# Gate stage of a two-layer encoder: its set-up and first two slices written inside the down projection's last group, and the gate product's first and last slices written in pairs

## The chip, the cores and the metric

The kernel runs on one core of one Trainium2 chip. The metric is the device time of a whole execution in microseconds (us), as the median of several runs.

## The reference

Two layers of an encoder block act on x, 1024 tokens of width 1024. Cut to what the kernel's stages need:

```
h = rmsnorm(x, g_pre_mix)
proj = h @ w_in                        # split in q, k, v, u, ... parts
y = concat(diff_attention(...), spatial_gating(b_u, b_v, ..., w_spatial, ...),
           window_gqa(...)) @ w_out
x = x + rmsnorm(y, g_post_mix)
gate, up = split(rmsnorm(x, g_pre_ffn) @ w_ffn_in)
f = (silu(gate) * up) @ w_ffn_out      # the down projection, 2816 -> 1024
x = x + rmsnorm(f, g_post_ffn)
e = p @ w_ple_up                       # p: 1024 x 256
g = sigmoid(rmsnorm(x, g_ple_gate) @ w_ple_gate)      # the gate product
x = x + rmsnorm(e * g, g_ple_post)
```

The gate stage is all that stands from the norm of f to the last line. It is run once in each layer.

## The kernel before

**Numbers.** Everything is float32. A product is made of three matmuls with the operands split into a high part (fp32r) and a low part (the rest): high x high, high x low, low x high. The two parts of an operand come from two instructions: ACT writes the high part (L209 for activations, L161 for weights, L819 for gate weights), VectorE subtracts it from the source and writes the low part (L210, L162, L820).

**Tiling.** The 1024 tokens are eight slices t of 128 rows. `T(t)` holds a slice in row form. `to_X` (L205) turns a slice into column form for use as a matmul's stationary operand: for each half of 512 columns it makes four transposes on TensorE into one bank of banks 4 to 7 (L202), then L209 and L210 read that bank. Which bank is taken is decided when the kernel is built: the one taken longest ago.

**The gate stage** (L807 to L884). Its set-up loads two gains, the column gain `gcol` and eight blocks of gate weights (L818), and converts them (L819, L820) into six tiles of pool W and two of pool F. For each slice the generator `ple` (L848) then has these steps:

- the norm of f (L850, with rows L194, L187, L189, L196), the load of the slice of x1 into `gv[:, 2]` (L852), the residual sum (L853), and the scaled copy `h1` (L855, L856);
- `to_X(h1)` (L858);
- the gate product `gmm(t)` (L864), its sigmoid on ACT (L866), the load of the slice of e into `gv[:, 3]` (L868), product (L869), norm, and the sum into `T(t)` (L871); then the store to x3 and, in layer 0, the norm for the next layer;
- in layer 0, `to_X(h2)` for the next layer's input (L880).

`gv[:, 2]` and `gv[:, 3]` are one buffer each: a slice's load waits until the slice before has been read. `gmm` is built by `rows_mm` (L223). When a slice is first asked for, it takes two banks of 0 to 3 and makes 48 matmuls of 128x512: for k from 0 to 7 six of them (L220), on two halves, with weight tile k.

**Around it.** Ahead stands the down projection: 11 groups c of two units, each over eight slices and two halves (L799), added by L805 into `T(t)`. Behind layer 0's gate stands the next layer's input product, called wb: the spatial weights are loaded into a buffer of the pool `raw` (L329) and turned by four transposes (L334). Eight blocks of w_in are loaded into `raw` (L173, three DMAs each) and converted into W (six) and F (two); `bmm` (L340) is the product by `rows_mm`. The projections (L238) come behind it.

**What sets the order.** The kernel isn't written in engine order. A scheduler simulates the program when it is built, hoists an instruction when its inputs and buffers are free, and fixes one order for each engine; the engines then run their rows strictly as they stand and wait on semaphores. The order in which the code is written is a priority, and it also decides the cycling of buffers and banks. Pools have a fixed number of buffers: W 6, F 2, raw 2, A 7, P 4, G 2.

Of the kernel before, what the change touches and what calls it, by code (L numbers as in the profile page):

```python
# [11 lines left out]
F32 = mybir.dt.float32  # L12
# [45 lines left out]
def encoder_kernel(  # L58
# [123 lines left out]
    def rows_unit(tag, w, k, eng=nc.vector, r=None, to=None):  # L182
        return unit(tag, lambda r: [(r, w[k * P : (k + 1) * P, :])], eng, r, to)
# [33 lines left out]
    def rows_step(ps, x, units, k, halves=(0, 1)):  # L217
        for a, b in ((0, 0), (0, 1), (1, 0)):
            for hf in halves:
                nc.tensor.matmul(ps[:, hf], x[a][:, k * P : (k + 1) * P], units[k][b][:, hf * 512 : (hf + 1) * 512],  # L220
                                 start=(k == 0 and a == 0 and b == 0), stop=(k == len(units) - 1 and a == 1))

    def rows_mm(units, x):  # L223
        done = {}

        def get(t):
            if t not in done:
                done[t] = pbank2()
                for k in range(len(units)):
                    rows_step(done[t], x(t), units, k)  # L230
            return done[t]

        return get
# [8 lines left out]
    def ple_prep(l, tags):  # L242
        pT = [pair("P") for _ in range(2)]
        for hf in range(2):
            pr = new(tags[hf], [P, 4, PLE])
            nc.sync.dma_start(pr, p[l, 0, hf * 512 : (hf + 1) * 512, :].rearrange("(t p) c -> p t c", p=P))
            for k in range(2):
                pp = pbank()
                for t in range(4):
                    nc.tensor.transpose(pp[:, t * P : (t + 1) * P], pr[:, t, k * P : (k + 1) * P], ident)  # L250
                hi = pT[k][0][:, hf * 512 : (hf + 1) * 512]
                nc.scalar.activation(hi, pp, AF.Copy)
                nc.vector.tensor_tensor(pT[k][1][:, hf * 512 : (hf + 1) * 512], pp, hi.bitcast(F32),
                                        op=ALU.subtract)
# [47 lines left out]
    for l in range(DEPTH):  # L302
# [34 lines left out]
        wb = wb if l == 0 else []  # L337
        while len(wb) < KT:
            wb.append(load_wb(l, len(wb)))
        bmm = rows_mm(wb, xt)  # L340
        V = region()

        def vt(t, c0, n):
# [438 lines left out]
                pass  # L782

        T = rows_regions()
        for c in range(ND // 2):
            if l > 0:
                if c == 1:
                    up = ple_prep(l, "GG")
                if 2 <= c < 2 + NT:
                    ple_up(l, c - 2, *up, "G")  # L790
            ds = (2 * c, 2 * c + 1)
            fs = [unit("FW"[c % 2], lambda r: [(r, f_d[l][d].rearrange("p a c -> p (a c)"))]) for d in ds]
            ws = [rows_unit("W", wfo, d) for d in ds]
            for t in range(NT):
                for hf in range(2):
                    po = pbank(range(8))
                    for i in range(2):
                        for a, b in ((0, 0), (0, 1), (1, 0)):
                            nc.tensor.matmul(po, fs[i][a][:, t * P : (t + 1) * P], ws[i][b][:, hf * 512 : (hf + 1) * 512],  # L799
                                             start=(i == 0 and a == 0 and b == 0), stop=(i == 1 and a == 1))  # L800
                    acc = T(t)[:, hf * 512 : (hf + 1) * 512]
                    if c == 0:
                        nc.scalar.activation(acc, po, AF.Copy)
                    else:
                        nc.vector.tensor_tensor(acc, po, acc, op=ALU.add)  # L805

        X, xt = x_regions()  # L807
        gv = region()
        gpo = gain("G", g_post_ffn, l)
        gcol = sb.tile([P, KT], F32, tag="gcol", name=nm("gcol"), bufs=1)  # L810
        nc.sync.dma_start(gcol, g_ple_gate[l].rearrange("(k p) -> p k", p=P))
        gpp = gain(None, g_ple_post, l, gv[:, 0])
        gnx = gain(None, g_pre_mix, l + 1, gv[:, 1]) if l + 1 < DEPTH else None
        wg = []
        for k in range(KT):

            r, w = new("raw", [P, 1024]), pair("W" if k < 6 else "F")
            nc.sync.dma_start(r, w_ple_gate[l, k * P : (k + 1) * P, :])  # L818
            nc.scalar.activation(w[0], r, AF.Copy, scale=gcol[:, k : k + 1])  # L819
            nc.vector.scalar_tensor_tensor(w[1], r, gcol[:, k : k + 1], w[0].bitcast(F32),  # L820
                                           op0=ALU.mult, op1=ALU.subtract)
            wg.append(w)
        gmm = rows_mm(wg, xt)

        def ple_tail(t):
            e, eg, y = gv[:, 1], new("G", [P, DM]), new("P", [P, DM])
            nc.sync.dma_start(e, e_d[l][t])
# [52 lines left out]
                to_X(h2, xt(t))  # L880
            yield

        for _ in skew(ple, NT, (2, 1, 0, -1)):
            pass  # L884


# [45 lines left out]
```

## Time and profile before

| | us |
|---|---|
| runs before, three: lowest, median, highest | 2720.49, 2721.49, 2722.28 |
| the profiled execution's own time | 2721.15 |
| its span on the profile's page | 2719.4 |
| gate product and wb product, TensorE busy in L220 with weights in W (1728 matmuls) | 419.5 |
| the same with weights in F (576 matmuls) | 148.1 |
| down projection, TensorE busy in L799 (both forms) | 263.7 and 220.0 |

The page describes one execution. It gives each engine's busy time, a chain of the work that ended last, and the costliest groups of instructions; further views show the rows of an engine in order of time, each with its start, its duration and, in brackets, the idle time ahead of it and what ended that, and the busy time of all engines in chosen windows. PE is TensorE, PEld its weight loads, DVE is VectorE, SP issues the DMAs. PEclk is the clock that TensorE was granted, 1.00 being full speed.

### The profile page before, as it was taken

To read this page: it belongs to the slowest core of one execution; us is meant where nothing else is said; L and a number is where in the kernel's file an instruction comes from. 1 tells how busy PE (TensorE), PEld (TensorE's weight loads), DVE (VectorE), ACT (ScalarE), POOL (GpSimd) and SP (SyncE) were. 2 spreads that over 40 slices of the span, in tenths; PEclk is the share of its full clock that TensorE was granted. 3 is DMA by queue.
4 is the path that set the end of the run, shared out by engine and by line. 5 is a ranking of instruction groups with operands and counts; after the bars stand their busy time and mean duration, and the time that the engine had idled before them with its cause. 6 is when DMAs were issued, how large, how long until landed. Compare 5 with 4: busy or idle time off the path is not lost.

```text
span 2719.4 us, 35553 instructions
## 1 busy us (share of the span) xinstructions
PE 2660.4 (98%) x13760; PEld 2140.7 (79%) x13760; DVE 1757.5 (65%) x2992; ACT 1143.2 (42%) x1911; POOL 319.3 (12%) x299
## 2 busy tenths in 40 slices
PE   8999999999999999999999999989999999999998
PEld 6887776778888888887878777668788888888877
DVE  5237698678666656767632677966866666466684
ACT  6126687543222223214521577854522222321253
POOL 1002335210000000001100223532000000000010
PEclk9999999999999999999999999999999999999999
DMA  6153402133232314334224323112323232332342
GB/s 238 28 155 92 110 2 71 71 95 94 85 93 71 93 69 150 99 101 136 93 82 116 94 71 93 30 57 86 101 93 93 70 93 74 132 125 104 132 131 78
DMA packets 193466, 258.38 MB, mean 95 GB/s; under 512 B 26513, under 2 KB 142737, under 8 KB 193297
## 3 DMA queue, kind: packets, MB, share of 16 engines
q1 hardware_dynamic: 193296, 256.11, 30.4%
q8 instruction: 108, 1.77, 0.3%
q14 instruction: 62, 0.50, 0.1%
HBM read 195.25 MB, written 60.82 MB: 94 GB/s over the span
## 4 chain that ended last, share of the span: by engine, by line
PE 91%; DVE 4%; ACT 2%; issue 1%; DMA 1%; POOL 1%; SPq 0%; DVEq 0%; POOLq 0%; ACTq 0%
PE banks L720 30%; PE banks L220 18%; PE banks L799 17%; PE banks L238 8%; PE banks L515 3%; PE banks L487 3%; PE banks L509 3%; PE banks L202 2%; PE banks L266 2%; PE banks L419 1%; PE banks L444 1%; PE banks L435 1%; PE banks L521 1%; DVE A L196 1%; DVE P L490 1%
## 5 line engine op out<-in xcount | busy, mean ns | idle before, releaser
L720 PE MATMUL banks<-A,W 128*128 128x512 f32 x3072 | 710.3, 391 | 7.4 <-ACT W L161 4.6
L720 PEld LDWEIGHTS banks<-A,W 128*128 128x128 f32 x3072 | 579.1, 189 | 131.4 <-ACT W L161 5.8
L220 PE MATMUL banks<-W,A 128*128 128x512 f32 x1728 | 419.5, 396 | 10.2 <-ACT A L209 6.0
L220 PEld LDWEIGHTS banks<-W,A 128*128 128x128 f32 x1728 | 324.3, 190 | 79.6 <-ACT A L209 7.3
L805 DVE TENSOR_TENSOR A<-banks,A 128x512 f32<-128x512 f32 x320 | 213.9, 687 | 109.6 <-PE banks L799 109.3
L799 PE MATMUL banks<-W,F 128*128 128x512 f32 x1152 | 263.7, 389 | 0.0
L799 PEld LDWEIGHTS banks<-W,F 128*128 128x128 f32 x1152 | 216.2, 188 | 44.9
L799 PE MATMUL banks<-W,W 128*128 128x512 f32 x960 | 220.0, 389 | 1.8 <-ACT W L161 1.8
L161 ACT ACTIVATE W<-G 128x1024 fp32r<-128x1024 f32 x88 | 92.5, 1060 | 296.7 <-PE banks L720 278.9
L189 POOL TENSOR_TENSOR stats<-stats,neghalf 128x1 f32<-128x1 f32 (+1 forms) x112 | 84.8, 759 | 1114.6 <-DVE stats L187 1113.8
L799 PEld LDWEIGHTS banks<-W,W 128*128 128x128 f32 x960 | 180.1, 188 | 39.4 <-ACT W L161 2.0
L161 ACT ACTIVATE W<-raw 128x1024 fp32r<-128x1024 f32 x92 | 96.6, 1060 | 208.6 <-PE banks L799 102.1
L238 PE MATMUL banks<-A,F 128*128 128x512 f32 x768 | 183.4, 393 | 0.0
L744 DVE TENSOR_TENSOR P<-banks,P 128x512 f32<-128x512 f32 x44 | 30.4, 691 | 219.8 <-PE banks L720 219.8
L238 PEld LDWEIGHTS banks<-A,F 128*128 128x128 f32 x768 | 142.3, 188 | 29.3 <-ACT G L428 0.3
L490 DVE CUSTOM_DVE_ANT_0 P<-banks,dist 128x1024 f32<-128x1024 f32 x116 | 139.8, 1219 | 32.5 <-PE banks L487 19.2
L220 PE MATMUL banks<-F,A 128*128 128x512 f32 x576 | 148.1, 400 | 2.7 <-DVE A L210 1.2
L493 ACT ACTIVATE P<-P,stats 128x1024 f32<-128x1024 f32 x116 | 133.1, 1149 | 30.5 <-DVE stats L490 26.9
L162 DVE TENSOR_TENSOR W<-raw,W 128x1024 fp32r<-128x1024 f32 x80 | 97.6, 1223 | 54.7 <-ACT W L161 54.4
L220 PEld LDWEIGHTS banks<-F,A 128*128 128x128 f32 x576 | 107.2, 191 | 25.8 <-DVE A L210 1.5
L720 PE MATMUL banks<-A,raw 128*128 128x512 f32 x528 | 126.8, 389 | 0.0
L511 ACT ACTIVATE PT<-banks 128x512 f32<-128x512 f32 x192 | 110.7, 591 | 30.6 <-PE banks L509 24.8
(193 smaller groups left out, 3851.5 us busy)
## 6 DMA issues: line engine op xcount, KB each, us to landing
F<-in_w_ffn_in_dram SPq DMA_DIRECT2D x88, 512.0 KB, 5.2
f<-P SPq DMA_DIRECT2D x44, 512.0 KB, 4.6
raw<-f SPq DMA_DIRECT2D x44, 512.0 KB, 3.3
raw<-in_w_ffn_out_dram SPq DMA_DIRECT2D x44, 512.0 KB, 3.5
W<-pre SPq DMA_DIRECT2D x64, 256.0 KB, 5.1
pre<-G SPq DMA_DIRECT2D x24, 512.0 KB, 3.5
x<-A SPq DMA_DIRECT2D x24, 512.0 KB, 2.6
e<-G SPq DMA_DIRECT2D x16, 512.0 KB, 4.9
```

The source lines that it names most:

```text
L161: nc.scalar.activation(hi, src, AF.Copy)
L162: eng.tensor_tensor(lo, src, hi.bitcast(F32), op=ALU.subtract)
L189: nc.gpsimd.tensor_tensor(r, v, neghalf[:, :k], op=ALU.pow)
L220: nc.tensor.matmul(ps[:, hf], x[a][:, k * P : (k + 1) * P], units[k][b][:, hf * 512 : (hf + 1) * 512], start=(k == 0 and a == 0 and b == 0 ...
L238: nc.tensor.matmul(po, w[a][:, k * P : (k + 1) * P], X[half][b][:, :, k * P : (k + 1) * P], start=(k == 0 and a == 0 and b == 0), stop=(k ...
L487: nc.tensor.matmul(sc[:, hf], slots[c][:, 0, t * P : (t + 1) * P], slots[c][:, 1, hf * 512 : (hf + 1) * 512], start=True, stop=True)
L490: nc.vector.tensor_tensor_reduce(pc, sc.rearrange("p a b -> p (a b)"), dist[:, 896 - 128 * t : 1920 - 128 * t], DIFF_SLOPES[h], HUGE, ALU. ...
L493: nc.scalar.activation(pc, pc, AF.Exp, bias=nmx[:, c : c + 1], scale=-1.0, accum_out=s[:, c : c + 1])
L511: nc.scalar.activation(pT_, pt, AF.Copy)
L720: nc.tensor.matmul(bank, w[i][a][:, k * P : (k + 1) * P], B[i][:, b, k * 512 : (k + 1) * 512], start=k == 0 and a + b == 0, stop=k == 3 an ...
L799: nc.tensor.matmul(po, fs[i][a][:, t * P : (t + 1) * P], ws[i][b][:, hf * 512 : (hf + 1) * 512], start=(i == 0 and a == 0 and b == 0), sto ...
L805: nc.vector.tensor_tensor(acc, po, acc, op=ALU.add)
```

## The change

The set-up, `ple_tail`, `ple` and the generator `ple_step = skew(ple, NT, (2, 1, 0, -1))` are now written ahead of or inside the down projection's loop: the set-up stands at the top of the last group c, and `next(ple_step)` is called there ahead of slices 2 and 5. So the first two steps of the stage (the norms of slices 0 and 1, and slice 0's `to_X`) are written among the last group's products. `rows_mm` takes a list of pairs: when a slice of a pair is first asked for, both of the pair get their banks, and the products are written k by k, six matmuls for the one slice and six for the other. The gate product has the pairs (0,1) and (6,7) in layer 0 and (0,1) in layer 1; wb's product has (0,1) in layer 1.

```diff
-    def rows_mm(units, x):
+    def rows_mm(units, x, pairs=()):
         done = {}
         def get(t):
             if t not in done:
-                done[t] = pbank2()
+                ts = next((q for q in pairs if t in q), (t,))
+                for i in ts:
+                    done[i] = pbank2()
                 for k in range(len(units)):
-                    rows_step(done[t], x(t), units, k)
+                    for i in ts:
+                        rows_step(done[i], x(i), units, k)
             return done[t]
...
-        bmm = rows_mm(wb, xt)
+        bmm = rows_mm(wb, xt, ((0, 1),) if l else ())
...
+        ple_step = skew(ple, NT, (2, 1, 0, -1))
         for c in range(ND // 2):
...
+            if c == ND // 2 - 1:
+                X, xt = x_regions()
+                gv = region()
+                gpo = gain("G", g_post_ffn, l)
...
+                gmm = rows_mm(wg, xt, ((0, 1), (6, 7)) if l + 1 < DEPTH else ((0, 1),))
             for t in range(NT):
+                if c == ND // 2 - 1 and t in (2, 5):
+                    next(ple_step)
                 for hf in range(2):
...
-        gmm = rows_mm(wg, xt)
...
-        for _ in skew(ple, NT, (2, 1, 0, -1)):
+        for _ in ple_step:
             pass
```

The instructions are the same in number and kind. In the compiled order the set-up and the norms stand at the same places on all engines as before. The pairs move rows at these places. (In the changed kernel's rows L817, L833 and L835 are the former L853, L869 and L871; L338, L334 and L335 are the former L334, L330 and L331; L837 is L873 and L832 is L868.)

**The start of layer 0's gate, TensorE.** The rows begin behind the last down product. P_778 and P_780 are `h1` of slices 0 and 1, W_762, W_764, W_766 the gate weights of k = 0, 1, 2, A_754 and A_755 the high and the low part of the column form of slices 0 to 3. Before:

```order
L202 MATMUL banks_63<-ident_65,P_778_9157 128x128 [waits DVE_49,Activation_49]
L202 MATMUL banks_63<-ident_65,P_778_9157 128x128 x3
L202 MATMUL banks_63<-ident_65,P_778_9157 128x128 [waits DVE_49]
L202 MATMUL banks_63<-ident_65,P_778_9157 128x128 x3
L220 MATMUL banks_63<-W_762_9111,A_754_9099 128x512 [waits Activation_49]
L220 MATMUL banks_63<-W_762_9111,A_754_9099 128x512 [waits DVE_49]
L220 MATMUL banks_63<-W_762_9111,A_754_9099 128x512 x2
L202 MATMUL banks_63<-ident_65,P_780_9169 128x128 [waits Activation_49]
L202 MATMUL banks_63<-ident_65,P_780_9169 128x128 x3
L202 MATMUL banks_63<-ident_65,P_780_9169 128x128 [waits DVE_49]
L202 MATMUL banks_63<-ident_65,P_780_9169 128x128 x3
L220 MATMUL banks_63<-W_762_9111,A_754_9099 128x512 [waits Activation_49]
```

With the change:

```order
L202 MATMUL banks_63<-ident_65,P_778_9073 128x128 [waits Activation_49]
L202 MATMUL banks_63<-ident_65,P_778_9073 128x128 x7
L220 MATMUL banks_63<-W_762_8999,A_754_8987 128x512 [waits DVE_49,Activation_49]
L220 MATMUL banks_63<-W_762_8999,A_754_8987 128x512 [waits DVE_49]
L220 MATMUL banks_63<-W_762_8999,A_754_8987 128x512 x2
L202 MATMUL banks_63<-ident_65,P_780_9127 128x128 [waits DVE_49,Activation_49]
L202 MATMUL banks_63<-ident_65,P_780_9127 128x128 x3
L220 MATMUL banks_63<-W_762_8999,A_755_8988 128x512 x2
L220 MATMUL banks_63<-W_764_9004,A_754_8987 128x512 x4
L220 MATMUL banks_63<-W_764_9004,A_755_8988 128x512 x2
L220 MATMUL banks_63<-W_766_9009,A_754_8987 128x512 x4
```

Before, the eight transposes of slice 1 stood behind slice 0's first four products and waited for ACT alone. Now four of them stand there, with a wait on VectorE also: they go into the bank that held slice 0's first half, which L210 has to have read. Slice 0's next products follow, and the other four transposes stand behind its products of k = 3.

**The same stage, VectorE.** A_665 is the half of T with slices 4 to 7, A_758 is `gv`. Before, from the residual sum of slice 4:

```order
L853 TENSOR_TENSOR A_665_7646<-A_665_7646,A_758_9103 128x1024
L210 TENSOR_TENSOR A_755_9100<-banks_63,A_754_9099 128x512 x2
L853 TENSOR_TENSOR A_665_7646<-A_665_7646,A_758_9103 128x1024
L869 TENSOR_TENSOR P_783_9258<-P_783_9258,A_758_9103 128x1024
L187 TENSOR_SCALAR stats_64<-stats_64 128x1
L853 TENSOR_TENSOR A_665_7646<-A_665_7646,A_758_9103 128x1024
L196 SCALAR_TENSOR_TENSOR P_783_9258<-P_783_9258,stats_64,A_758_9103 128x1024
L871 TENSOR_TENSOR A_664_7645<-A_664_7645,P_783_9258 128x1024
L853 TENSOR_TENSOR A_665_7646<-A_665_7646,A_758_9103 128x1024
```

With the change, from the same sum:

```order
L817 TENSOR_TENSOR A_665_7646<-A_665_7646,A_758_8991 128x1024
L210 TENSOR_TENSOR A_755_8988<-banks_63,A_754_8987 128x512
L817 TENSOR_TENSOR A_665_7646<-A_665_7646,A_758_8991 128x1024 x3
L833 TENSOR_TENSOR P_783_9306<-P_783_9306,A_758_8991 128x1024
L210 TENSOR_TENSOR A_755_8988<-banks_63,A_754_8987 128x512 x2
L187 TENSOR_SCALAR stats_64<-stats_64 128x1
L196 SCALAR_TENSOR_TENSOR P_783_9306<-P_783_9306,stats_64,A_758_8991 128x1024
L835 TENSOR_TENSOR A_664_7645<-A_664_7645,P_783_9306 128x1024
```

Before, the two L210 of slice 2's column form stood ahead of the sums of slices 5, 6 and 7 (not shown is that slice 1's stand further up). Now one L210 of slice 1 and the sums of slices 5, 6 and 7 (three rows in one) and L869 stand ahead of slice 2's two.

**The hand-over to wb's product, TensorE.** raw_811 holds the spatial weights; W_817, W_819, W_821, W_823 are wb's weights of k = 2, 3, 4, 5. Before:

```order
L220 MATMUL banks_63<-W_817_9985,A_754_9099 128x512 x6
L220 MATMUL banks_63<-W_817_9985,A_755_9100 128x512 x2
L220 MATMUL banks_63<-W_817_9985,A_754_9099 128x512 x2
L220 MATMUL banks_63<-W_817_9985,A_755_9100 128x512 x2
L334 MATMUL banks_63<-ident_65,raw_811_9958 128x128 x4
L220 MATMUL banks_63<-W_819_9992,A_754_9099 128x512 x6
L220 MATMUL banks_63<-W_819_9992,A_755_9100 128x512 x2
L220 MATMUL banks_63<-W_819_9992,A_754_9099 128x512 x2
L220 MATMUL banks_63<-W_819_9992,A_755_9100 128x512 x2
```

With the change:

```order
L220 MATMUL banks_63<-W_821_9999,A_754_8987 128x512 x4
L220 MATMUL banks_63<-W_821_9999,A_755_8988 128x512 x2
L220 MATMUL banks_63<-W_821_9999,A_754_8987 128x512 x4
L220 MATMUL banks_63<-W_821_9999,A_755_8988 128x512 x2
L338 MATMUL banks_63<-ident_65,raw_811_9958 128x128 x4
L220 MATMUL banks_63<-W_823_10006,A_754_8987 128x512 x6
L220 MATMUL banks_63<-W_823_10006,A_755_8988 128x512 x2
L220 MATMUL banks_63<-W_823_10006,A_754_8987 128x512 x2
```

The four transposes that read raw_811, and so set its buffer free, stood ahead of the products with W_819 before; now they stand ahead of those with W_823, two weight tiles later.

**The same place, SP's DMA queue.** raw_820 to raw_826 are the raw blocks of k = 4 to 7. Before:

```order
L173 DMA raw_820_9995<-in_w_in_dram 128x384 [waits PE_49]
L173 DMA raw_820_9995<-in_w_in_dram 128x128
L173 DMA raw_820_9995<-in_w_in_dram 128x512 [waits DMAHW2_49]
L173 DMA raw_822_10002<-in_w_in_dram 128x384 [waits DMAHW4_49,DMAHW3_49,DVE_49]
L173 DMA raw_822_10002<-in_w_in_dram 128x128
L173 DMA raw_822_10002<-in_w_in_dram 128x512 [waits DMAHW5_49]
L173 DMA raw_824_10009<-in_w_in_dram 128x384 [waits DMAHW2_49,DMAHW1_49,DMAHW6_49,DMAHW0_49,DVE_49]
L173 DMA raw_824_10009<-in_w_in_dram 128x128 [waits DMAHW7_49]
L173 DMA raw_824_10009<-in_w_in_dram 128x512
```

With the change:

```order
L173 DMA raw_822_10002<-in_w_in_dram 128x384 [waits DMAHW6_49,DMAHW7_49,DMAHW5_49,DVE_49]
L173 DMA raw_822_10002<-in_w_in_dram 128x128
L173 DMA raw_822_10002<-in_w_in_dram 128x512 [waits DMAHW2_49]
L837 DMA x3_0_7_112<-A_665_7646 128x1024 [waits DVE_49]
L334 DMA P_810_9957<-in_gmlp_ln_g_dram 128x256 [waits DMAHW4_49,PE_49]
L335 DMA P_810_9957<-in_gmlp_ln_b_dram 128x256
L173 DMA raw_824_10009<-in_w_in_dram 128x384 [waits DMAHW1_49,DMAHW2_49,DMAHW0_49,DVE_49]
L173 DMA raw_824_10009<-in_w_in_dram 128x128
L173 DMA raw_824_10009<-in_w_in_dram 128x512
L173 DMA raw_826_10016<-in_w_in_dram 128x384 [waits PE_49]
```

The load that waits for TensorE (PE in its brackets) is the one that takes raw_811's buffer: raw_820 before, raw_826 now. The others wait for the conversion of the block before them in the other buffer (VectorE).

More of the change, by code (lines that the diff above doesn't have):

```diff
@@ L784, in encoder_kernel @@
         T = rows_regions()
[L785 to L822, printed above, removed]
-        gmm = rows_mm(wg, xt)
         def ple_tail(t):
@@ L881, in ple @@
             yield
-        for _ in skew(ple, NT, (2, 1, 0, -1)):
+        ple_step = skew(ple, NT, (2, 1, 0, -1))
+        for c in range(ND // 2):
+            if l > 0:
+                if c == 1:
+                    up = ple_prep(l, "GG")
+                if 2 <= c < 2 + NT:
+                    ple_up(l, c - 2, *up, "G")
+            ds = (2 * c, 2 * c + 1)
+            fs = [unit("FW"[c % 2], lambda r: [(r, f_d[l][d].rearrange("p a c -> p (a c)"))]) for d in ds]
+            ws = [rows_unit("W", wfo, d) for d in ds]
+            if c == ND // 2 - 1:
+                X, xt = x_regions()
+                gv = region()
+                gpo = gain("G", g_post_ffn, l)
+                gcol = sb.tile([P, KT], F32, tag="gcol", name=nm("gcol"), bufs=1)
+                nc.sync.dma_start(gcol, g_ple_gate[l].rearrange("(k p) -> p k", p=P))
+                gpp = gain(None, g_ple_post, l, gv[:, 0])
+                gnx = gain(None, g_pre_mix, l + 1, gv[:, 1]) if l + 1 < DEPTH else None
+                wg = []
+                for k in range(KT):
+                    r, w = new("raw", [P, 1024]), pair("W" if k < 6 else "F")
+                    nc.sync.dma_start(r, w_ple_gate[l, k * P : (k + 1) * P, :])
+                    nc.scalar.activation(w[0], r, AF.Copy, scale=gcol[:, k : k + 1])
+                    nc.vector.scalar_tensor_tensor(w[1], r, gcol[:, k : k + 1], w[0].bitcast(F32),
+                                                   op0=ALU.mult, op1=ALU.subtract)
+                    wg.append(w)
+                gmm = rows_mm(wg, xt, ((0, 1), (6, 7)) if l + 1 < DEPTH else ((0, 1),))
+            for t in range(NT):
+                if c == ND // 2 - 1 and t in (2, 5):
+                    next(ple_step)
+                for hf in range(2):
+                    po = pbank(range(8))
+                    for i in range(2):
+                        for a, b in ((0, 0), (0, 1), (1, 0)):
+                            nc.tensor.matmul(po, fs[i][a][:, t * P : (t + 1) * P], ws[i][b][:, hf * 512 : (hf + 1) * 512],
+                                             start=(i == 0 and a == 0 and b == 0), stop=(i == 1 and a == 1))
+                    acc = T(t)[:, hf * 512 : (hf + 1) * 512]
+                    if c == 0:
+                        nc.scalar.activation(acc, po, AF.Copy)
+                    else:
+                        nc.vector.tensor_tensor(acc, po, acc, op=ALU.add)
```

## The prediction

> **What bounds the kernel now.** I read first the busy times, the span and the chain that ended last, on the profile's page.
>
> ```profile
> span 2719.4 us, 35553 instructions
> PE 2660.4 (98%) x13760; PEld 2140.7 (79%) x13760; DVE 1757.5 (65%) x2992; ACT 1143.2 (42%) x1911; POOL 319.3 (12%) x299
> PE 91%; DVE 4%; ACT 2%; issue 1%; DMA 1%; POOL 1%; SPq 0%; DVEq 0%; POOLq 0%; ACTq 0%
> ```
>
> TensorE is busy for 2660.4 of 2719.4 us, so all that can be won in the whole program is 59 us. The change leaves the count of matmuls alone. It can only move TensorE's idle time, and the stretches of low clock that follow idle time. So the second view is the busy time by stretch, for the gate stage of layer 0, the hand-over to the next layer's input product (called wb below), the packed stretch behind it, and the gate stage of layer 1.
>
> ```profile
> core 0: us, PE busy (x) PEld busy (x) DVE busy (x) ACT busy (x) POOL busy (x), PEclk, DMA share, GB/s
> 1255.30:1363.60 108.30, 104.91 (x506) 87.10 (x504) 75.58 (x101) 62.15 (x94) 17.09 (x25) 0.97 0.35 117
> 1363.60:1393.00 29.40, 25.66 (x112) 20.08 (x111) 14.90 (x16) 11.92 (x19) 1.10 (x2) 0.94 0.54 155
> 1393.00:1458.30 65.30, 65.30 (x289) 54.07 (x288) 17.09 (x45) 8.54 (x17) 4.02 (x7) 1.00 0.08 20
> 2609.50:2711.50 102.00, 97.51 (x451) 79.91 (x450) 58.23 (x75) 45.12 (x68) 13.35 (x18) 0.98 0.30 104
> ```
>
> Idle are 3.39 us in the gate of layer 0, 3.74 in the hand-over, none from 1393.00 to 1458.30, and 4.49 in the gate of layer 1. Together that is 11.6 us, less than half a per cent. Whatever arrives late at 1393.00 is not recovered behind it, since nothing idles there.
>
> **The set-up costs nothing and brings nothing.** Written earlier, the gains, the gate weights and the norms of slices 0 and 1 stand in the compiled order of each engine, SP's and POOL's too, where they stood before: the scheduler had already hoisted them, and slice 0's transposes still come behind the last down product. I take 0 us. Only the pairing moves instructions.
>
> **The pair (0,1) at the start of layer 0's gate.** Here are five rows of TensorE's timeline (start, duration, engine, line; in brackets the idle time ahead and what ended it), then four of VectorE's.
>
> ```profile
> 1255.85 1.03 PE L202 MATMUL banks<-ident,P 128*128 128x128 f32 x8
> 1258.09 1.19 PE L220 MATMUL banks<-W,A 128*128 128x512 f32 x4 [1.20 <-ACT A L209]
> 1260.65 1.74 PE L202 MATMUL banks<-ident,P 128*128 128x128 f32 x8 [1.37 <-ACT P L856]
> 1263.21 10.59 PE L220 MATMUL banks<-W,A 128*128 128x512 f32 x36 [0.82 <-ACT A L209]
> 1287.27 8.33 PE L220 MATMUL banks<-W,A 128*128 128x512 f32 x36
> ...
> 1262.86 0.69 DVE L210 TENSOR_TENSOR A<-banks,A 128x512 fp32r<-128x512 f32 x1
> 1283.00 1.23 DVE L853 TENSOR_TENSOR A<-A,A 128x1024 f32<-128x1024 f32 x1 [0.20 <-DMA A<-x]
> 1288.48 1.23 DVE L853 TENSOR_TENSOR A<-A,A 128x1024 f32<-128x1024 f32 x1 [1.80 <-DMA A<-x]
> 1291.70 1.22 DVE L869 TENSOR_TENSOR P<-P,A 128x1024 f32<-128x1024 f32 x1
> ```
>
> A matmul's pitch at full clock is 8.33/36, about 0.23 us. The same 36 took 10.59 at 1263.21, because a half-clock stretch lay over their beginning.
>
> (a) Before, all eight transposes of slice 1 ran at 1260.65, into two banks that were free, and the stage ran on from 1263.21. In the changed order four of them take the bank of slice 0's first half again, so they wait for that half's low part, the L210 that ends at 1262.86 + 0.69 = 1263.55. The whole gate product is queued behind them on TensorE. Then the eight transposes are still to be paid, 1.74, up to about 1265.3, where before the matmuls had begun at 1263.21: 2.1 us, in a stretch at half clock in both kernels, so about half of it in work, **+1.1**. Bounds: 0 (if slice 0's ready products fill it) to 2.1.
>
> (b) The transposes of slice 2 stand behind the pair's last matmul and no longer among the products, so the conversion of their first half, some 0.6 on ACT, is bare but for the second half's transposes: +0.35 (0 to 0.6).
>
> (c) Slice 2's low part now stands on VectorE behind the residual sums (L853) of slices 5, 6 and 7, and an L869. Those sums go through one buffer for the x1 slices, each waiting for the next load: 1283.00 and 1288.48 are the last two of before. With the last at 1288.0, L869 ends near 1290.3 and the first L210 near 1290.9. Before, slice 2 began at 1287.27 and had its four high products done 0.9 later, at 1288.2. So the low products start **+2.7** late. This is a wait for a clock time, so it swallows (a) and (b). If the x1 chain is no limit, 1.45 of (a) and (b) stay; if it runs as late as before's own 1288.48 and the norm's row comes between, 4.
>
> (d) Slice 3's conversions queue behind the tails of slices 0 and 1 that now come together, one VectorE row of 1.2 to 1.3: +1.3 (0 to 1.6).
>
> The middle of the gate is late by 2.7 + 1.3 = **4.0** (1.5 to 5). Nothing there wins it back, since the rest of that stage is busy.
>
> The clock there is a row of its own, three windows of layer 0 and three of layer 1:
>
> ```profile
> 1257.52:1260.93 3.41, 1.48 (x7) 0.96 (x8) 3.41 (x6) 3.41 (x7) 1.64 (x2) 1.00 0.35 89
> 1260.93:1267.76 6.83, 6.01 (x19) 4.68 (x18) 6.83 (x11) 4.27 (x8) 2.52 (x3) 0.50 0.60 196
> 1267.76:1274.58 6.82, 6.82 (x32) 5.61 (x31) 6.00 (x6) 1.78 (x2) 0.00 (x0) 1.00 0.59 173
> 2612.61:2616.03 3.42, 2.29 (x12) 1.53 (x12) 3.42 (x5) 3.42 (x8) 0.72 (x1) 1.00 0.55 161
> 2616.03:2619.44 3.41, 1.61 (x6) 1.05 (x7) 3.41 (x5) 2.23 (x5) 1.52 (x1) 1.00 0.83 232
> 2619.44:2622.85 3.41, 3.41 (x10) 2.64 (x9) 3.41 (x7) 2.15 (x3) 1.98 (x2) 0.50 0.50 161
> ```
>
> A window with 1.48 or 1.61 us of work is followed by 0.50, one with 2.29 is not, and a full one ends it. Each half-clock window that is filled with work costs 3.41/2 = 1.7. [...]
>
> **The hand-over to wb.** First TensorE's rows, then the eight conversions of wb's weights on ACT.
>
> ```profile
> 1350.69 3.79 PE L220 MATMUL banks<-W,A 128*128 128x512 f32 x16
> 1371.52 0.60 PE L334 MATMUL banks<-ident,raw 128*128 128x128 f32 x4
> 1380.16 7.34 PE L220 MATMUL banks<-W,A 128*128 128x512 f32 x24 [2.84 <-ACT W L161]
> 1387.34 5.84 PE L220 MATMUL banks<-F,A 128*128 128x512 f32 x24
> ...
> 1352.25 1.06 ACT L161 ACTIVATE W<-raw 128x1024 fp32r<-128x1024 f32 x1 [0.33 <-PE banks L220]
> 1359.24 1.06 ACT L161 ACTIVATE W<-raw 128x1024 fp32r<-128x1024 f32 x1 [3.20 <-DMA raw<-in_w_in_dram]
> 1365.53 1.06 ACT L161 ACTIVATE W<-raw 128x1024 fp32r<-128x1024 f32 x1 [1.84 <-DMA raw<-in_w_in_dram]
> 1371.85 1.06 ACT L161 ACTIVATE W<-raw 128x1024 fp32r<-128x1024 f32 x1 [3.25 <-DMA raw<-in_w_in_dram]
> 1379.05 1.06 ACT L161 ACTIVATE W<-raw 128x1024 fp32r<-128x1024 f32 x1 [0.98 <-DMA raw<-in_w_in_dram]
> 1380.38 1.06 ACT L161 ACTIVATE W<-raw 128x1024 fp32r<-128x1024 f32 x1 [0.27 <-DMA raw<-in_w_in_dram]
> 1385.98 1.06 ACT L161 ACTIVATE F<-raw 128x1024 fp32r<-128x1024 f32 x1 [4.54 <-DMA raw<-in_w_in_dram]
> 1387.38 1.06 ACT L161 ACTIVATE F<-raw 128x1024 fp32r<-128x1024 f32 x1 [0.34 <-DMA raw<-in_w_in_dram]
> ```
>
> The pool `raw` has two buffers, and the spatial weights hold one until L334's four transposes have read them. Up to then the wb loads go one at a time through the other; behind it they go in twos. Before, those transposes ran at 1371.52, ahead of the fourth unit's products, and the eight conversions show it: four singly, then two twos. That is five rounds behind the first: 6.99, 6.29, 6.32, 7.20 and 6.93, 33.7 in all, 6.75 each.
>
> In the changed order the four transposes stand two units later, behind the products of the fifth unit. So six conversions go singly and only the last two together: **six rounds**. The first conversion waits for slice 7's first products (six behind 1350.69) to release their W buffer. It comes 4.0 later by the gate, and 1.4 sooner because pairing (6,7) puts that product six matmuls earlier: 1352.25 + 2.65 = 1354.9. Six rounds of 6.75 lead to 1395.4, and the eighth conversion 1.4 behind it, 1396.8, against 1387.38: **+9.4**. A round can also grow: in three of before's first conversions ACT stood idle for 1.8 to 3.3 until the load landed, whereas with the tails of slices 6 and 7 in a pair an ACT row of about 1.05 will stand ahead of some. And TensorE will idle some 10 us more in this stretch, so one half-clock window may fall on the last 24 products (1.7). For both I take +1.1, between 0 and 3. The cover that is gone is the gate's own work: before, 24 products behind 1380.16 lay beside the last load round, and now TensorE waits. The start of the packed stretch moves by 9.4 + 1.1 = **+10.5** (7 to 13), and by the row of 1393.00 all of it stays.
>
> **The pair (0,1) in layer 1's gate.**
>
> ```profile
> 2613.29 1.19 PE L220 MATMUL banks<-W,A 128*128 128x512 f32 x4 [2.24 <-ACT A L209]
> 2614.82 1.09 PE L202 MATMUL banks<-ident,P 128*128 128x128 f32 x8 [0.33 <-ACT P L856]
> 2617.37 1.19 PE L220 MATMUL banks<-W,A 128*128 128x512 f32 x4 [1.46 <-ACT A L209]
> 2619.02 9.16 PE L220 MATMUL banks<-W,A 128*128 128x512 f32 x32 [0.46 <-DVE A L210]
> ...
> 2618.28 1.28 DVE L210 TENSOR_TENSOR A<-banks,A 128x512 fp32r<-128x512 f32 x2
> ```
>
> The order is the same as in layer 0. Slice 1's transposes can't run at 2614.82; they wait for slice 0's L210, the first of the two from 2618.28 (or sooner by one L196, 1.27, that stood ahead of it: 2617.8). Then the eight transposes and slice 1's first four products, 1.09 + 1.19, are still to do, beside which only the wait to 2619.02 falls away: about **+1.4**, the half clock being there in both. The bare conversion at the pair's end adds 0.8 (0.35 to 1.2). I take **+2.2** (0.6 to 3). Some rows around the attention's output product in layer 1 also change places; with TensorE busy on both sides I take 0 (-1.5 to 1.5).
>
> **Sum.** 10.5 + 2.2 = 12.7 on the profiled execution's own 2721.15 gives 2733.9. That execution lies 0.34 below the median 2721.49, so no correction is made.
>
> **Rivals.**
>
> 1. The pairing fills the waits: **faster**. It decides at the start of both gates: the second slice's transposes would have to start by 1260.65, so the low half of slice 0 would have to be converted by then and not at 1263.55. If so, the waits 1.37, 0.82, 0.33, 1.46 and 0.46 go, as do two half-clock windows of 1.7 and the hand-over's 2.84: near 2710. Against it stands VectorE, without a gap from 1257.52 to 1267.76 (3.41 and 6.83 busy). Chance 0.04.
> 2. The sixth round is hidden, because loads in the thinner traffic come in under 5.6 us each. Then the gate's 4.0 meet the hand-over's idle 3.74, and a layer 1 of +2.2 and some 2 are left: 2725.5 (2723 to 2727). Against it: rounds of 6.29 are the shortest of five. Chance 0.12, of it three quarters within 0.2%.
> 3. The rounds stretch to 7.7, each conversion one ACT row of 1.05 later: 6 x 0.95 = 5.7 less the 1.1 already taken: 2738.5. For it: ACT will do two tails at once. Chance 0.20.
> 4. TensorE takes ready products ahead of a waiting transpose, so the new bank wait costs nothing: 10.5 less the gate's 4.0 gives 2727.7. Against it: before 1263.21 it idled 0.82, with the next weights ready. [...] Chance 0.04.
>
> **How the numbers follow.** The forecast, both new waits and the sixth round, has 0.60: 2730 to 2737. Rival 3 reaches to 2740, rivals 2 and 4 end near 2727. From 2727 to 2740 about 0.8 is held. A measurement of this kernel tells about 0.2%, 5.4 us, from no change; so faster 0.04, same 0.09 (most of rival 2), slower 0.87.
>
> **What would show it.** (i) A wait of about 3 to 4 us of the second L202 row on VectorE's L210 near 1259 to 1263.6, with 0.50 behind it. (ii) Slice 2's low products waiting 1 to 3 us on L210 near 1291. (iii) Seven moments of wb conversion in place of six, the two with F near 1395.4 and 1396.8. (iv) The first L238 about 10.5 later. (v) Layer 1's gate about 2 longer. The prediction is wrong if the wb loads go in twos before the fifth unit, if they land faster when alone, or if idle time before 1350 absorbs the 4.0.

## The result and the profile after

The changed kernel takes 2733.88 us (median of 4 runs, 2731.96 to 2735.1); the kernel before took 2720.99 beside it (4 runs, 2719.66 to 2722.28). The ratio is 1.005, with a 95% interval from 1.0038 to 1.0063: 12.9 us slower. The forecast was 2733.9, and its range held the time. The total is right, its terms are not: two were too small by 3.7 us together, and a stage that the forecast held at nothing came out 3.4 shorter.

The page of the changed kernel, whose profiled execution took 2733.07:

```profile
span 2731.3 us, 35558 instructions
PE 2660.6 (97%) x13760; PEld 2139.4 (78%) x13760; DVE 1758.9 (64%) x2992; ACT 1141.8 (42%) x1911; POOL 323.8 (12%) x299
```

TensorE is busy for as long as before (2660.6 against 2660.4) in a span that is 11.9 longer. Busy time by stretch, the columns as before: the gate of layer 0, the hand-over to wb, the packed stretch, the gate of layer 1, then seven windows of the clock.

```profile
1254.98:1366.23 111.25, 103.47 (x489) 85.28 (x488) 69.09 (x92) 56.92 (x87) 18.60 (x23) 0.95 0.32 104
1366.23:1405.91 39.68, 30.50 (x125) 22.70 (x124) 20.96 (x24) 15.72 (x25) 2.20 (x4) 0.87 0.48 146
1405.91:1471.19 65.28, 65.28 (x289) 54.05 (x288) 17.10 (x45) 8.53 (x16) 4.04 (x7) 1.00 0.07 17
2619.27:2723.61 104.34, 97.42 (x449) 80.13 (x447) 57.90 (x73) 44.88 (x68) 13.08 (x18) 0.97 0.29 101
1255.98:1259.40 3.42, 1.23 (x5) 0.67 (x4) 3.42 (x5) 3.42 (x6) 2.32 (x2) 1.00 0.16 31
1259.40:1266.23 6.83, 3.41 (x10) 2.90 (x11) 6.83 (x11) 4.04 (x8) 2.11 (x3) 0.50 0.69 217
1300.39:1303.80 3.41, 1.64 (x9) 0.87 (x6) 3.07 (x5) 1.43 (x3) 0.30 (x1) 0.99 0.44 154
1303.80:1307.21 3.41, 3.35 (x8) 2.70 (x9) 2.13 (x5) 2.24 (x5) 0.55 (x1) 0.50 0.38 154
1375.44:1382.27 6.83, 4.21 (x9) 2.94 (x10) 3.61 (x4) 3.00 (x4) 0.55 (x1) 0.50 0.48 153
1395.89:1399.30 3.41, 1.30 (x10) 0.98 (x9) 0.62 (x1) 1.59 (x3) 0.00 (x0) 1.00 0.67 223
1399.30:1402.71 3.41, 3.41 (x10) 2.41 (x9) 2.94 (x4) 1.49 (x2) 0.00 (x0) 0.51 0.42 122
```

Idle time in layer 0 grew from 3.4 + 3.7 to 7.8 + 9.2 us. Half-clock windows of 3.41 us there went from three to six: one is new behind the window with 1.64 us of work and one behind that with 1.30, and from 1375.44 there are two (0.50) in place of the one that the kernel before has at 1380.40 (0.50). The packed stretch is as long as before and wins nothing back.

A stage's length is read from the starts of its first rows in TensorE's timeline. In the order of time: the first gate starts 0.87 sooner than before (1254.98); from there to the projections (first L238, now L242) it is 216.21 against 202.45, **+13.76**; layer 1's attention, to the first FFN product, 454.70 against 458.10, **-3.40**; its FFN -0.24; layer 1's gate 104.34 against 101.72, **+2.62**. The sum is 11.87, the difference of the ends.

TensorE's rows at the start of layer 0's gate, then VectorE's, in the changed kernel:

```profile
1254.98 1.03 PE L202 MATMUL banks<-ident,P 128*128 128x128 f32 x8
1262.82 1.09 PE L202 MATMUL banks<-ident,P 128*128 128x128 f32 x4 [4.41 <-DVE A L210]
1287.53 8.83 PE L220 MATMUL banks<-W,A 128*128 128x512 f32 x36 [0.25 <-ACT A L209]
1301.38 1.19 PE L220 MATMUL banks<-W,A 128*128 128x512 f32 x4 [0.55 <-ACT A L209]
1303.86 9.08 PE L220 MATMUL banks<-W,A 128*128 128x512 f32 x32 [1.29 <-DVE A L210]
...
1261.99 0.68 DVE L210 TENSOR_TENSOR A<-banks,A 128x512 fp32r<-128x512 f32 x1
1285.78 1.23 DVE L817 TENSOR_TENSOR A<-A,A 128x1024 f32<-128x1024 f32 x1 [3.40 <-DMA A<-x]
1288.06 1.28 DVE L210 TENSOR_TENSOR A<-banks,A 128x512 fp32r<-128x512 f32 x2
```

The first wait is the forecast one: 4.41 us for L210, whose end at 1262.67 lets slice 1's transposes go. At slice 2 TensorE waits hardly at all, since the last x1 sum came at 1285.78. The larger loss is at slice 3: 0.55, 1.29 and the half clock (0.50) from 1303.80.

ACT's conversions of wb's weights, and TensorE's rows beside them:

```profile
1355.55 1.06 ACT L161 ACTIVATE W<-raw 128x1024 fp32r<-128x1024 f32 x1 [2.96 <-PE banks L220]
1361.99 1.06 ACT L161 ACTIVATE W<-raw 128x1024 fp32r<-128x1024 f32 x1 [5.38 <-DMA raw<-in_w_in_dram]
1368.64 1.06 ACT L161 ACTIVATE W<-raw 128x1024 fp32r<-128x1024 f32 x1 [2.54 <-DMA raw<-in_w_in_dram]
1376.91 1.06 ACT L161 ACTIVATE W<-raw 128x1024 fp32r<-128x1024 f32 x1 [5.21 <-DMA raw<-in_w_in_dram]
1384.67 1.06 ACT L161 ACTIVATE W<-raw 128x1024 fp32r<-128x1024 f32 x1 [4.75 <-DMA raw<-in_w_in_dram]
1391.12 1.06 ACT L161 ACTIVATE W<-raw 128x1024 fp32r<-128x1024 f32 x1 [3.35 <-DMA raw<-in_w_in_dram]
1397.59 1.06 ACT L161 ACTIVATE F<-raw 128x1024 fp32r<-128x1024 f32 x1 [3.89 <-DMA raw<-in_w_in_dram]
1399.25 1.06 ACT L161 ACTIVATE F<-raw 128x1024 fp32r<-128x1024 f32 x1
...
1378.02 8.19 PE L220 MATMUL banks<-W,A 128*128 128x512 f32 x25 [5.81 <-ACT W L161]
1390.92 0.66 PE L338 MATMUL banks<-ident,raw 128*128 128x128 f32 x4
1398.70 7.38 PE L220 MATMUL banks<-F,A 128*128 128x512 f32 x24 [2.10 <-ACT F L161]
```

Six conversions come singly, at distances of 6.4 to 8.3 us, and a couple only at the end, behind the transposes at 1390.92: six rounds, 42.0 us in all, where five took 33.7. The last 24 products then take 7.38 in place of 5.84; from 1399.30 to 1402.71 they were granted 0.51, and 1.00 throughout before.

### The profile page after: what moved, and what is told of

Same layout as the page of the kernel before. It is cut to its first block, busy times and chain, and to the rows that moved or that the text cites. A ratio compares the mean times of both kernels' runs of the same rounds, so it can differ in the third digit from the quotient of the medians.

```text
span 2731.3 us, 35558 instructions
## 1 busy us (share of the span) xinstructions
PE 2660.6 (97%) x13760; PEld 2139.4 (78%) x13760; DVE 1758.9 (64%) x2992; ACT 1141.8 (42%) x1911; POOL 323.8 (12%) x299
## 4 chain that ended last, share of the span: by engine, by line
PE 88%; DVE 5%; ACT 2%; issue 2%; DMA 1%; POOL 1%; SPq 0%; DVEq 0%; POOLq 0%; ACTq 0%
PE banks L724 30%; PE banks L220 17%; PE banks L883 16%; PE banks L242 8%; PE banks L519 3%; PE banks L491 3%; PE banks L513 3%; PE banks L202 2%; PE banks L270 2%; PE banks L423 1%; PE banks L448 1%; PE banks L439 1%; DMA raw<-in_w_in_dram 1%; DVE A L196 1%; PE banks L525 1%
## 5 line engine op out<-in xcount | busy, mean ns | idle before, releaser
L242 PE MATMUL banks<-A,F 128*128 128x512 f32 x768 | 183.3, 393 | 0.0
L242 PEld LDWEIGHTS banks<-A,F 128*128 128x128 f32 x768 | 142.3, 188 | 29.3 <-ACT G L432 0.3
```

Of the source, the lines that this page charges most:

```text
L242: nc.tensor.matmul(po, w[a][:, k * P : (k + 1) * P], X[half][b][:, :, k * P : (k + 1) * P], start=(k == 0 and a == 0 and b == 0), stop=(k ...
```

## The experiments

Every run's stage length is the stretch from the first L202 behind layer 0's down projection to the first projection of layer 1, called "layer 0" in this table, and the length of layer 1's gate stage to TensorE's last matmul. Times are medians; the kernel before was run beside each of them. The two lengths are those of one profiled execution, and in e11 and e12, the same two programs again, they differ from the first profiles by up to 1.3 us (layer 0) and 1.8 us (gate 1).

| kernel | time (before beside it) | ratio, 95% interval | layer 0 | gate 1 |
|---|---|---|---|---|
| before | 2720.99 | | 202.45 | 101.72 |
| changed | 2733.88 (2720.99) | 1.0050 [1.0038, 1.0063] | 216.21 | 104.34 |
| e1 set-up only | 2724.04 (2719.94) | 1.0012 [1.0003, 1.0021] | 203.91 | 102.70 |
| e2 pairs only | 2733.19 (2719.94) | 1.0045 [1.0033, 1.0058] | 213.13 | 103.15 |
| e3 set-up, layer 0's (0,1) | 2726.56 (2719.94) | 1.0026 [1.0015, 1.0036] | 208.23 | 103.05 |
| e4 set-up, layer 0's (6,7) | 2721.21 (2719.94) | 1.0004 [0.9996, 1.0013] | 201.79 | 102.42 |
| e5 changed, own banks | 2731.84 (2720.43) | 1.0043 [1.0031, 1.0056] | 214.34 | 102.71 |
| e6 changed, own buffer | 2726.71 (2720.43) | 1.0024 [1.0015, 1.0032] | 206.41 | 104.66 |
| e7 changed, both edits | 2726.12 (2720.43) | 1.0020 [1.0011, 1.0029] | 206.46 | 104.00 |
| e8 before, own buffer | 2712.08 (2720.43) | 0.9972 [0.9961, 0.9983] | 195.59 | 101.15 |
| e9 both edits, only (6,7) | 2711.52 (2719.00) | 0.9971 [0.9960, 0.9982] | 194.67 | 99.19 |
| e10 both edits, only (0,1) | 2716.19 (2719.00) | 0.9989 [0.9980, 0.9998] | 199.57 | 102.11 |
| e11 before again | 2720.99, one run | | 202.23 | 99.92 |
| e12 changed again | 2734.49, one run | | 214.91 | 103.67 |

**e1: the set-up alone.**

```diff
-        bmm = rows_mm(wb, xt, ((0, 1),) if l else ())
+        bmm = rows_mm(wb, xt)
...
-                gmm = rows_mm(wg, xt, ((0, 1), (6, 7)) if l + 1 < DEPTH else ((0, 1),))
+                gmm = rows_mm(wg, xt)
```

> The set-up and the first two steps stay inside the last group of the down projection; all three lists of pairs are empty. The kernel's order now shows four of slice 1's transposes in the bank of slice 0's first half, with a wait on VectorE, in this kernel too, and wb's loads in five rounds, as before. Theory (the late gate has its cause in that bank, which comes from where slice 1's to_X is written; the big loss is the sixth round, which needs the pairs): a wait of about 4.4 us on L210 ahead of slice 1's transposes in both gates, the first conversion of wb 1 to 3 us later, five rounds, the first L242 0 to 3 us later against the gate's start, layer 1's gate 1 to 2 longer, time 2721 to 2725. Rival (as the prediction had it, the pairs alone move instructions): no such wait, both gates as before, 2721 within 1.5.

TensorE's second row of transposes in layer 0's gate, in e1:

```profile
1265.47 1.09 PE L202 MATMUL banks<-ident,P 128*128 128x128 f32 x4 [4.40 <-DVE A L210]
```

The wait is there without any pair, so it belongs to the set-up's place: banks are handed out in the order in which code is written. It is cheap: +1.5 in layer 0, since the kernel before waits there as well (1.37 and 0.82), and about +1 in layer 1's gate. Both are near what two profiles of one program differ by. In layer 1's gate the idle time is the firmer figure: 4.49 us in the kernel before and 4.48 in e11, 5.61 in e1. As a whole e1 is 1.0003 to 1.0021 of the kernel before.

**e2: the pairs alone**, in the kernel before (the set-up behind the down projection, `rows_mm` and its lists as in the change).

> The three lists of pairs are as in the change; the set-up and the first steps stand behind the down projection, as before. Its order has no wait for slice 0's bank, but six rounds of wb loads. Theory (sixth round): about 10 to 12 of the change's 12.9 us remain: slice 1's transposes start where they did before, conversions in seven moments, the first L242 10 to 12 us later against the gate's start, layer 1's gate within 0 to 2 of before; 2730 to 2733. Rival (the late gate and its bank wait carry the loss, the rounds only follow it): with the bank wait gone the loss goes too, and 2721 to 2725 is left.

The same row in e2, and its last two conversions of wb on ACT:

```profile
1259.95 1.97 PE L202 MATMUL banks<-ident,P 128*128 128x128 f32 x8 [1.37 <-ACT P L860]
...
1395.97 1.06 ACT L161 ACTIVATE F<-raw 128x1024 fp32r<-128x1024 f32 x1 [4.36 <-DMA raw<-in_w_in_dram]
1397.88 1.06 ACT L161 ACTIVATE F<-raw 128x1024 fp32r<-128x1024 f32 x1
```

The bank wait is gone, the six rounds remain (first conversion 1354.59, last 1397.88: 43.3), and 10.7 of the 13.8 us of layer 0 with them. The rival falls. (The time, 2733.19, is 0.2 above the range expected.)

**e3 and e4: one pair each** (the list of layer 0 cut to (0,1), or to (6,7); none in layer 1 and wb).

> The set-up as in the change, and of the pairs only (0,1) of layer 0's gate; layer 1 and wb have none. Its order has the bank wait and five rounds. Theory (sixth round): the gate's middle is 4 to 6 us late as in the changed kernel, but wb's weights come in five rounds, so the first L242 is 3 to 6 late against the gate's start; 2723 to 2727. Rival (the first pair's bare conversions are the loss, whatever the rounds): 2731 to 2734.

> The set-up as in the change, and of the pairs only (6,7) of layer 0's gate. Its order has the bank wait at the gate's start, and the spatial weights' transposes one unit earlier than before (ahead of the third unit's products), five rounds. Theory (sixth round, which needs both pairs together): the first L242 0 to 3 us late against the gate's start, 2721 to 2725, beside the set-up alone within 1.5. Rival (the last pair by itself delays the hand-over, since ACT has two slices' tails at once): 2729 to 2734.

Beside the set-up alone, the first pair costs 4.3 in layer 0 and the last one gains 2.1, more than the 1.5 either way that was expected. (Two profiles of one program differ by up to 1.3 in this stretch, e11 and e12.) With the set-up's 1.5 that would be +3.7 against the kernel before, and the change has +13.8. The rest, some 10 us, appears with neither pair alone: in both runs wb's weights come in five rounds, and only with both pairs do the spatial weights' transposes fall behind the fifth unit. (These two runs also lack the pairs in layer 1's gate and in wb's product; no run takes wb's pair out alone.)

**e5: own banks.**

```diff
-    def to_X(src, dst):
+    def to_X(src, dst, among=range(4, 8)):
...
-            to_X(h1, xt(t))
+            to_X(h1, xt(t), ((4, 5), (6, 7))[t] if t < 2 else range(4, 8))
```

> The changed kernel, but slice 0's two halves of transposes are told to take banks 4 and 5, slice 1's banks 6 and 7, in both gates. The wait of slice 1's transposes on VectorE goes from the order; the six rounds stay. Theory (sixth round dominates, the bank wait is a part of the gate's lateness of 4 to 5 us): the 4.4 us wait is gone, the first conversion of wb comes 1 to 3 earlier than in the changed kernel, the first L242 stays 9 to 12 late against the gate's start, layer 1's gate 1 to 2 shorter than in the changed kernel; 2729 to 2733. Rival (the bank wait is what costs): within 2 of before, 2719 to 2723.

**e6: own buffer for the spatial weights.**

```diff
-        wsr = new("raw", [P, 1024])
+        wsr = new("raw" if l == 0 else "G", [P, 1024])
```

> The changed kernel, but in layer 1 the spatial weights are loaded into a buffer of the pool G and no longer into one of the two of raw. So wb's loads go in twos from the first on; the bank wait stays. Theory (sixth round): the eight conversions of wb take about 20 us from first to last, in place of 43.7, the last wait of TensorE ahead of wb's F products goes, and the first L242 is 1 to 5 late against the gate's start: 8 to 11 less than the changed kernel, 2722 to 2726. Rival (the loads are limited by the DMA queues and not by the buffers, or the pair's tails on ACT limit the conversions): the rounds stretch to twice their length, and 2731 to 2735 stays.

Removing the 4.4 us wait wins about 2 us of time, with intervals that overlap, and 1.9 of layer 0. Removing the sixth round, by one tile's pool, wins 9.8 of layer 0 and 7 of time (e6's time is 0.7 above the range expected, and the conversions take 24.2 us and not about 20). Four of e6's conversions, the first two and the last two:

```profile
1355.62 1.06 ACT L161 ACTIVATE W<-raw 128x1024 fp32r<-128x1024 f32 x1 [2.93 <-PE banks L220]
1356.98 1.06 ACT L161 ACTIVATE W<-raw 128x1024 fp32r<-128x1024 f32 x1 [0.30 <-PE banks L220]
...
1376.90 1.06 ACT L161 ACTIVATE F<-raw 128x1024 fp32r<-128x1024 f32 x1 [4.16 <-DMA raw<-in_w_in_dram]
1379.81 1.04 ACT L161 ACTIVATE F<-raw 128x1024 fp32r<-128x1024 f32 x1
```

All eight take 24.2 us from first to last, against 43.7. Between the two pairs shown lie three rounds of two loads, (1376.90 - 1355.62)/3 = 7.1 us each; the changed kernel's six, five of them of a single load, took 7.0. So it is the buffer that limits, not the bytes.

**e7 and e8: both edits on the change; the buffer on the kernel before.**

> The changed kernel with both edits: banks 4 to 7 apart for slices 0 and 1, and the spatial weights in G. Theory (bank wait and sixth round together hold all of layer 0's loss): the first L242 within -1 to 3 of before against the gate's start, layer 1's gate 1 to 2 longer than before for the bare conversion at the pair's end; 2719 to 2724. Rival (what is left of the pairing, bare conversions and two tails at once, costs as much by itself): 2726 to 2731.

> The kernel before, with the spatial weights of layer 1 in a buffer of G; set-up and pairs as before. Theory (one raw buffer that is held makes the rounds, five of them before): the idle 3.7 us of the hand-over go, with a half-clock window of 1.7, so the first L238 comes 4 to 7 sooner; 2714 to 2718, faster than both kernels. Rival (five rounds were hidden under the gate's own work, so a free buffer brings nothing until there is a sixth): 2720 to 2722.

e8 is faster than both kernels, by more than expected: five rounds had not been hidden either. Its layer 0 is 6.9 shorter than that of the kernel before. e7 went the rival's way: with both causes gone the pairing still costs 10.9 in layer 0 against e8. And with the buffer free the bank wait costs nothing that these profiles show: e6, which has it, is at 206.41, and e7, which hasn't, at 206.46. TensorE's waits in e7 behind the first pair, and one in the hand-over:

```profile
1287.90 8.46 PE L220 MATMUL banks<-W,A 128*128 128x512 f32 x36 [0.25 <-ACT A L209]
1302.23 1.20 PE L220 MATMUL banks<-W,A 128*128 128x512 f32 x4 [1.40 <-ACT A L209]
1304.37 7.55 PE L220 MATMUL banks<-W,A 128*128 128x512 f32 x32 [0.94 <-DVE A L210]
1318.44 7.10 PE L220 MATMUL banks<-W,A 128*128 128x512 f32 x30 [1.12 <-DVE A L210]
...
1379.08 0.73 PE L220 MATMUL banks<-F,A 128*128 128x512 f32 x2 [2.23 <-ACT F L161]
```

The first four are 3.7 us for conversions of slices 2 to 4, none of which the kernel before or e8 has. Slices 0 and 1 end together, so no products are left to lie beside the next slices' transposes and conversions. The last row is the longest of three waits in the hand-over, 3.3 us together, for the conversions of wb's weights; e8, e9 and e10 have none there. The other 3.9 of the 10.9 us is longer busy time of the same matmuls. One half-clock window more than in e8, at 1380.44 (the four products from 1380.34 took 2.00 us, four at 1302.23 took 1.20), makes up to 1.7 of it, an estimate from half of its 3.41; the rest stays open.

**e9 and e10: both edits with one pair each.**

> Both edits of e7 (own banks for slices 0 and 1, spatial weights in G), set-up as in the change, and of the pairs only (6,7) of layer 0. It asks which pair holds the 10.9 us by which e7's layer 0 (206.46) is longer than that of the kernel before with the buffer alone (195.59). Theory (the first pair, with conversions that TensorE waits for at its end): without it layer 0's stretch from the gate to the first L242 is 194 to 198, layer 1's gate 101 to 102.5, time 2711 to 2716. Rival (the last pair, whose two tails come at once in the hand-over): 202 to 206, time 2719 to 2724.

> As the run before, but of the pairs only (0,1) of layer 0. Theory (the first pair): TensorE waits 2.5 to 4 us for conversions of slices 2, 3 and 4, as in e7, and layer 0's stretch is 201 to 206; time 2717 to 2723. Rival (the last pair): 195 to 198, time 2711 to 2716. If both pairs share it, each of the two runs lies between.

With the last pair alone layer 0 is 0.9 shorter than in e8, with the first pair alone 4.0 longer. So e9 lies where the first pair was blamed (but for layer 1's gate, 99.19, below the 101 expected), and e10 (199.57, and 2716.19 in time) between the two theories, with waits for conversions of 2.6 us (e10's profiled execution, 2720.72, is the longest of its eleven). Together the pairs cost 10.9, 7.8 more than the sum. Here is layer 0's stretch in e8, e9, e10 and e7:

```profile
1254.65:1450.24 195.59, 192.43 (x902) 159.89 (x900) 106.53 (x160) 81.95 (x127) 22.04 (x34) 0.98 0.29 93
1256.73:1451.40 194.67, 190.00 (x901) 157.83 (x900) 106.32 (x160) 81.22 (x127) 21.97 (x34) 1.00 0.29 94
1257.96:1457.53 199.57, 192.11 (x902) 159.03 (x900) 106.60 (x160) 81.06 (x127) 23.86 (x34) 0.99 0.29 91
1256.32:1462.78 206.46, 196.30 (x901) 160.86 (x900) 106.85 (x160) 80.88 (x127) 22.92 (x34) 0.98 0.27 88
```

TensorE idles there for 3.2, 4.7, 7.5 and 10.2 us. In waits, then, the last pair costs 1.5, the first 4.3 and both 7.0, only 1.2 more than the sum. The rest of the 7.8 is busy time of the same matmuls, and most of that goes with the granted clock: e9 has no half-clock window in this stretch (1.00 granted over it), e10 one (0.99), e8 two and e7 three (0.98 both). Whether the pairs bring these windows, or the moment at which an execution reaches the stage, these profiles don't separate. e9's time can't be told from e8's.

**e11 and e12: the two kernels again.**

> The kernel before once more, for a second profile of the same program. It asks how far a stage's length differs between executions. If the attention stage of layer 1 (458.10 before, 454.70 with the change) differs by chance, this one will lie anywhere from 454.5 to 458.5, and so will layer 0's (455.24); if the change shortens it, 457.5 to 458.7. The gate stretch of layer 0 within 1.5 of 202.45, layer 1's gate within 0.7 of 101.72.

> The changed kernel once more, for the same question: attention stage of layer 1 454.5 to 458.5 if by chance, 454 to 455.3 if the change shortens it. The gate stretch of layer 0 within 1.5 of 216.21, layer 1's gate within 0.7 of 104.34; conversions of wb in seven moments.

The attention of layer 1 in the two profiles of the kernel before, 458.10 and 459.52, and of the changed one, 454.70 and 455.93 (busy times in the stretch; the first two lines are the kernel before):

```profile
1458.30:1916.40 458.10, 446.36 (x2949) 341.15 (x2948) 314.25 (x704) 276.51 (x553) 129.05 (x103) 0.99 0.30 85
```

```profile
1458.88:1918.40 459.52, 448.77 (x2950) 342.87 (x2948) 313.66 (x704) 276.95 (x553) 129.27 (x103) 0.99 0.29 84
```

```profile
1471.19:1925.89 454.70, 444.54 (x2949) 340.22 (x2948) 313.73 (x704) 275.81 (x553) 130.75 (x103) 1.00 0.30 85
```

```profile
1472.64:1928.57 455.93, 445.82 (x2950) 341.29 (x2949) 314.31 (x704) 275.91 (x554) 130.71 (x103) 0.99 0.30 85
```

The second profile of the kernel before lies above both ranges expected, that of the changed one in the range for chance alone. (Layer 1's gate, 99.92 in e11, also lies outside its 0.7.) The same work keeps TensorE busy for 444.5 to 448.8 us. Of the 3.4 us between the first profiles 1.8 are busy time, of the 3.6 between the second 3.0; that goes with the clock, which had two and four half-clock windows in the kernel before, one and two in the changed (0.96 and 0.93, 0.98 and 0.96 granted over the fourth fifth of the stage, 1.00 elsewhere). The rest (10.2 and 10.1 idle against 11.7 and 10.7) is waiting. e5 and e8, whose order there is all but that of the kernel before, show 455.83 and 455.88, so one order ranges over 3.7 us, and most of the shorter stage doesn't need the changed one. Layer 0's attention, the same rows in all kernels, ranges from 454.3 to 457.0 over the fourteen profiles. Whether the change itself gives the 3.4 back, or the moment at which the stage starts, stays open.

## Why the forecast came out

**The sixth round: right, and the chief term.** The 33.7 us of five rounds became 42.0, by 8.3; e6 showed that the one buffer holds them. But the step named the pairs (6,7) and the late gate only for the first conversion; that neither pair alone brings the sixth round, e3 and e4 showed.

**The set-up "costs nothing and brings nothing; only the pairing moves instructions": wrong.** e1 has the bank wait, e2 hasn't. I had laid it to the pair, and so had the text on the change, which lists these transposes among the rows that the pairs move. The wait itself is 4.41 us, where the prediction had 3 to 4. Its price is +1.5 in layer 0 and some +1 in layer 1, within what the prediction booked under the pair.

**The gate's middle, +4.0: too small; it is +5.5.** At the end of slice 5 the changed kernel stands 87.7 us behind its start, where the kernel before stood at 82.2 (the products behind that slice's F rows start at 1342.67 and 1338.02). Term (c), the 2.7 for slice 2's low part, failed: the last x1 sum came at 1285.78, which is 1286.65 if the gate's earlier start is added, and not at 1288.0. Term (d), 1.3, was too small: slice 3 waits 1.84, and behind that wait stands a half-clock window (0.50 from 1303.80 to 1307.21), 1.7 by half of its 3.41, which I had priced but not put there. The first conversion came 4.2 late and not 2.65.

**The hand-over, +10.5: in place +13.76 in layer 0**, above its bound of 13, and +12.68 in the second profiles (e12 against e11), below it. In the first, the last 24 products start 12.2 later against the gate's start, by the 4.2 and the 8.3, and took 1.5 longer themselves (7.38 against 5.84, with 0.51 granted from 1399.30 to 1402.71); +1.1 for this and the longer rounds together was too little.

**Layer 1's gate, +2.2: right in its waits.** The length moved by +2.62 in the first profiles and by +3.75, above the bound of 3, in the second. But TensorE's idle time there is 4.49 and 4.48 in the kernel before, 6.92 in both profiles of the changed: +2.4, of which the bank wait makes 1.1 (e1 has 5.61) and a wait of 1.31 for the bare conversion behind the pair the rest, where 1.4 and 0.8 had been taken. What is more or less than 2.4 in the length goes with the granted clock (0.98 and 1.00 before, 0.97 twice with the change). The wait behind the pair, in the changed kernel:

```profile
2653.39 6.88 PE L220 MATMUL banks<-W,A 128*128 128x512 f32 x29 [1.31 <-ACT A L209]
```

**Layer 1's attention, 0 (-1.5 to 1.5): wrong**, -3.4 and -3.6. This error and the 3.7 us too few in the hand-over's and layer 1's gate's terms cancel, and that the sum hit so closely is luck: the stages add up to 11.9 in the profiled execution (the first gate's earlier start and the FFN take 1.1 more), and the median lies 0.8 above that execution.

**The rivals.** The pairing fills no waits (rival 1). The sixth round is not hidden (rival 2), and the rounds grew to 7.0 and not to 7.7 (rival 3). TensorE did not pass its waiting transposes (rival 4): it stood 4.41 us. (The price of rival 4, 2727.7, leaves out all of layer 1's +2.2, though only 1.4 of it was the bank wait.)

## What to carry to other kernels

Where a pool has two buffers, look who holds one and when it is set free: a small tile that waits for its reader halves the pool for all loads behind it, and a change far off can move that reader. Ending two slices together leaves nothing to lie beside the next slice's transposes and conversions (3.7 us of waits in e7). A sum that hits is no proof of its terms: compare stage by stage.

## What was not expected of the hardware

Waits of the same length were followed by half clock in e2 and not in e5. Here are the gate's second transposes and the first long row of products, in e2 and then in e5:

```profile
1262.51 10.36 PE L220 MATMUL banks<-W,A 128*128 128x512 f32 x36 [0.59 <-ACT A L209]
```

```profile
1261.08 1.09 PE L202 MATMUL banks<-ident,P 128*128 128x128 f32 x8 [1.35 <-ACT P L820]
1263.64 8.45 PE L220 MATMUL banks<-W,A 128*128 128x512 f32 x36 [1.47 <-ACT A L209]
```

And the clock's windows over them, two of e2 and one of e5:

```profile
1256.39:1259.80 3.41, 1.19 (x4) 0.67 (x4) 3.41 (x6) 3.41 (x7) 2.08 (x2) 1.00 0.22 60
1259.80:1263.21 3.41, 2.67 (x10) 2.17 (x11) 3.41 (x5) 3.15 (x7) 0.00 (x0) 0.50 0.71 243
```

```profile
1259.01:1262.42 3.41, 1.81 (x12) 1.08 (x10) 3.41 (x5) 3.41 (x7) 0.58 (x1) 1.00 0.57 174
```

Ahead of these transposes both waited alike, 1.37 (e2's row stands above) and 1.35 us. Yet they ran for 1.97 in e2 and for 1.09 in e5, and the 36 products for 10.36 and 8.45. In e2 one window holds only 1.19 us of work, and 0.50 follows. In e5 the windows lie otherwise over the same waits: the emptiest holds 1.81, and the clock stays at 1.00. In the changed kernel 0.50 also followed a window with 1.64 us of work out of 3.41 (1300.39). So, as far as these windows show, where waits of 1.37 and 1.35 us fell among them decided whether another 1.7 was lost, an estimate from half of 3.41.
